# Gates, branch projections and merge with tokens on partitions; attention values placed behind fill work

## The chip, the cores and the metric

The kernel runs on one core of a Trainium2 chip. The metric is the device time of one execution in microseconds (us), as the median of three runs. A core has TensorE (PE; its weight loads are PEld), VectorE (DVE), ScalarE (ACT), GpSimd (POOL) and SyncE (SP), which run their own instruction streams and wait for one another by semaphores.

## What is computed

One layer of a diffusion backbone: 256 latent tokens and 256 context tokens, width 2048, all fp32. The part that the change touches, cut from the reference:

```python
proj = h @ w_in[l]          # columns: q 512 | kv 256 + rotary 64 | u 1024 | v 1024 | gates 4096
...
g = sigmoid(gate_in)
merged = g[..., :D_MODEL] * (attn_o @ w_br_attn) + g[..., D_MODEL:] * (sgu_o @ w_br_sgu)
x = x + g1 * (merged @ w_out)
```

`attn_o` (256 x 1024) is the output of 8 heads that attend to 512 keys; `sgu_o` (256 x 1024) is the output of the spatial gating unit. Ahead of it stand RMSNorm and a modulation by shift and scale from `silu(c) @ w_mod`; behind it a second norm, modulated by the second half of the same map (here "modulation 2": shift, gate, scale and gate of 2048 each), and a SwiGLU of width 5632.

## The kernel before

Every product of activations and weights is made of two-part numbers: a value is split into `hi` (fp32r) and `lo` (the rest, fp32r), and a product is three matmuls, hi·hi, hi·lo and lo·hi (`mm3`, all matmuls at L255). Class `W` loads weights in pieces of 512 KB (`raw`, ten buffers, on SP's queue, L234); each 512 columns of a piece become a `whi` by a copy on ACT (L241) and a `wlo` by a subtraction on DVE (L242), eight buffers of each. Four such parts, 1 MB, are one `W`. 

A product can stand in PE two ways. In the F form a 128x128 weight tile is the stationary operand and the 256 tokens move, so the result has features on its partitions: 256 columns for each matmul (`mm3`), or, in `mm_wides`, hi and lo of the tokens side by side as 512 columns for the weight's hi and 256 for its lo, which leaves two sums in one PSUM bank that the eviction adds (L641 copies on ACT, L642 adds on DVE). In the T form 128 tokens of activations are stationary and 512 columns of weights move; the result has tokens on its partitions.

The stages in the profile: input projection with modulation 1 (0 to 222 us; `in_chunk`, T items for q and v, F tiles for u and the first 4 of 32 gate tiles), the spatial gating unit and the up-projections UQ, UK, UV (222 to 346), attention (346 to 496), SGU branch projection (496 to 543), attention branch projection with the merge (543 to 591), `wout` (592 to 681), norm, SwiGLU in (692 to 1180) and out (to the end). The 28 remaining gate tiles are *fill work*: `fill_items` yields 28 half items of one `W` each, which `fill` interleaves with the stages from SGU to attention (2 in each of the 8 attention steps), then the 8 SGU branch items, whose product is multiplied into `gate_b` (L654). Attention runs 8 steps, each 4 head pairs x 2 halves of the queries: `softmax` (scores, maximum with the key row on DVE L827, exponential on ACT L833, reciprocal and scaling L834 and L835), `weighted` of the step before (four 128x128 transposes on PE L844 for each of two heads, their copy to SBUF on ACT L846, and, every second step, the products with the values and their split L290/L291), then the fill work.

Modulation 2 is *background* work: a row of 1024 columns is accumulated on DVE, 16 pieces of 512 KB each (L425, L427), at a rate per fill item. Where a row is done, four matmuls sum it over partitions, ACT copies the sums into a slot `e` (L447), POOL sends them in four DMAs to DRAM (L450) and by DMA back in the wanted layout, and `MOD2_DUE` pieces later the bias is added. The slots (`slot()`) are a pool of 60 buffers of 128x512: a new owner of a buffer waits for the last use of the old one, DMAs among them.

The order of each engine's instructions is fixed when the kernel is built, by a scheduler that goes by the order of the code, its dependences and its pools; the waits are put in then. PSUM is 4 banks "mm" and 4 banks "aux".

Of the kernel before, what the change touches and what calls it, by code (L numbers as in the profile page):

```python
# [13 lines left out]
P = 128  # L14
# [32 lines left out]
MOD2_DUE = 7  # L47
# [21 lines left out]
NB_Q, NB_V = 1, 2  # L69
NB_T = NB_Q + NB_V  # L70
NT_U, NT_G = 8, 32
KV_COLS = KV_LORA + ROPE

NT_GE = 4
NT_F = NT_U + NT_GE

# [46 lines left out]
def block_kernel(  # L123
# [277 lines left out]
    def mod2_items():  # L401


        due = []
# [209 lines left out]
    acc_v = acc_t[NB_Q:]  # L614
# [3 lines left out]
    gate_a, gate_b = acc[NT_U // 2:], []  # L618
    sgo = []
    raw_gates = list(gate_a)  # L620
# [217 lines left out]
    def weighted(p, qt):  # L838
# [22 lines left out]
    for i, (p, qt) in enumerate(steps):  # L861
# [5 lines left out]
        fill(ATT_GATES[i], ATT_RATE)  # L867
# [320 lines left out]
```

## Time and profile before

| | us |
|---|---|
| three runs | 1429.76, 1432.1, 1434.71 |
| median | 1432.1 |
| profiled execution | 1430.99 |
| span of the profiled execution | 1429.2 |
| PE busy in it | 1402.0 (98%) |
| DVE busy | 1009.3 (71%) |
| ACT busy | 766.6 (54%) |

The profiled execution lies 1.1 us under the median and 1.8 us over its own span. Busy PE is not PE at its peak: consecutive matmuls overlap, so that the cost of a matmul is read from start to start, not from its own duration.

### The profile page before, as it was taken

Reading aid. Unit: us, or ns where it says so; the run is one execution under the profiler, and the core shown is the slowest. Engines: PE = TensorE matmul, PEld = TensorE weight load, DVE = VectorE, ACT = ScalarE, POOL = GpSimd, SP = SyncE. Lnnn points to the kernel's source line nnn. Section 1 sums busy time; section 2 is a strip of 40 time slices with the busy share of each in tenths; the row PEclk is TensorE's granted clock in tenths of the full one; section 3 lists DMA queues with packets and bytes.
Section 4 is the critical chain, followed back from the end, with each engine's and each line's share of the span. In section 5 each row is a group of like instructions: output and inputs, shape, how many; then the busy total and the mean of one; then the engine's idle time right before and its main releaser. Section 6 shows DMA issues by size and latency. Waiting matters only on the chain.

```text
span 1429.2 us, 23093 instructions
## 1 busy us (share of the span) xinstructions
PE 1402.0 (98%) x8390; PEld 1189.0 (83%) x8390; DVE 1009.3 (71%) x1748; ACT 766.6 (54%) x1438; POOL 21.9 (2%) x44
## 2 busy tenths in 40 slices
PE   6999999999999999999999999999999999999998
PEld 3887899995867899888888888888888888888886
DVE  2677687984898779997766666666666667786553
ACT  4655466564645745554665555555555554444442
POOL 0000000001100000000000000000000000000000
PEclk9999999999999999999999999999999999999999
DMA  9987877674797798897444555555555568898560
GB/s 369 362 315 294 344 275 238 245 271 146 241 364 278 271 348 331 299 396 270 148 162 163 190 186 185 192 192 190 187 184 192 192 217 305 303 373 303 191 207 31
DMA packets 104019, 355.50 MB, mean 249 GB/s; under 512 B 12504, under 2 KB 14936, under 8 KB 103904
## 3 DMA queue, kind: packets, MB, share of 16 engines
q1 hardware_dynamic: 101952, 350.30, 67.5%
q0 software_dynamic: 1952, 3.72, 0.9%
q8 instruction: 66, 1.08, 0.3%
q14 instruction: 49, 0.40, 0.1%
HBM read 351.83 MB, written 2.13 MB: 248 GB/s over the span
## 4 chain that ended last, share of the span: by engine, by line
PE 91%; DMA 4%; DVE 3%; ACT 1%; issue 1%; SPq 0%; POOL 0%; DVEq 0%; ACTq 0%
PE mm L255 86%; PE ax L255 5%; DMA raw<-in_wmod_dram 2%; DVE acc L427 1%; DMA raw<-in_win_dram 1%; DVE wlo L242 1%; DMA m_d<-g 0%; ACT whi L241 0%; DMA g<-in_xT_dram 0%; ACT g L386 0%; DMA raw<-in_wbrs_dram 0%; DMA raw<-in_wkv_dram 0%; PE ax L844 0%; PE ax L359 0%; DVE g L827 0%
## 5 line engine op out<-in xcount | busy, mean ns | idle before, releaser
L241 ACT ACTIVATE whi<-raw 128x512 fp32r<-128x512 f32 (+1 forms) x900 | 556.4, 628 | 490.1 <-PE mm L255 363.4
L242 DVE TENSOR_TENSOR wlo<-raw,whi 128x512 fp32r<-128x512 f32 (+1 forms) x900 | 605.5, 687 | 271.2 <-ACT whi L241 261.7
L255 PE MATMUL mm<-g,whi 128*128 128x512 f32 (+1 forms) x2880 | 767.7, 358 | 0.0
L255 PE MATMUL mm<-g,wlo 128*128 128x256 f32 x2368 | 504.8, 281 | 0.6 <-DVE wlo L242 0.6
L255 PEld LDWEIGHTS mm<-g,wlo 128*128 128x128 f32 x2368 | 438.8, 189 | 79.4 <-issue 1.3
L255 PEld LDWEIGHTS mm<-g,whi 128*128 128x128 f32 x2880 | 447.9, 190 | 9.9 <-issue 3.3
L255 PE MATMUL mm<-whi,g 128*128 128x512 f32 (+1 forms) x1312 | 400.9, 385 | 1.9 <-ACT whi L241 1.1
L255 PEld LDWEIGHTS mm<-whi,g 128*128 128x128 f32 x1312 | 244.2, 188 | 53.6 <-issue 3.7
L255 PE MATMUL mm<-wlo,g 128*128 128x512 f32 (+1 forms) x656 | 251.0, 383 | 0.5 <-DVE wlo L242 0.5
L427 DVE SCALAR_TENSOR_TENSOR acc<-raw,silw,acc 128x1024 f32<-128x1024 f32 x120 | 153.8, 1282 | 19.3 <-DMA raw<-in_wmod_dram 18.6
L255 PEld LDWEIGHTS mm<-wlo,g 128*128 128x128 f32 x656 | 123.5, 188 | 24.9 <-DVE wlo L242 2.1
L561 DVE TENSOR_TENSOR g<-mm,g 128x512 f32<-128x512 f32 (+1 forms) x72 | 46.4, 655 | 23.4 <-PE mm L255 22.9
L255 PE MATMUL ax<-g,g 128*128 128x128 f32 (+2 forms) x224 | 45.8, 384 | 3.8 <-ACT g L846 3.4
L290 ACT ACTIVATE g<-g 128x256 fp32r<-128x256 f32 x100 | 39.0, 411 | 13.9 <-DVE g L1024 8.2
L1021 ACT ACTIVATE g<-mm 128x256 f32<-128x256 f32 x88 | 29.0, 382 | 30.9 <-PE mm L255 30.9
L1022 DVE TENSOR_TENSOR g<-mm,g 128x256 f32<-128x256 f32 x88 | 33.2, 419 | 17.3 <-ACT g L1021 17.2
L291 DVE TENSOR_TENSOR g<-g,g 128x256 fp32r<-128x256 f32 x100 | 40.2, 420 | 7.2 <-ACT g L290 7.0
L255 PEld LDWEIGHTS ax<-g,g 128*128 128x128 f32 (+1 forms) x224 | 28.4, 195 | 17.1 <-issue 9.3
L255 PE MATMUL ax<-raw,silw 128*32 128x256 f32 (+1 forms) x576 | 31.8, 358 | 4.1 <-DMA raw<-in_wmod_dram 4.0
L255 PEld LDWEIGHTS ax<-raw,silw 128*32 128x32 f32 x576 | 16.9, 109 | 17.0 <-DMA raw<-in_wmod_dram 6.6
L386 ACT ACTIVATE g<-g,m 128x256 f32<-128x256 f32 x32 | 17.6, 593 | 9.7 <-DVE m L375 5.3
L1024 DVE TENSOR_TENSOR g<-g 128x256 f32<-128x256 f32 x44 | 18.4, 419 | 1.0 <-ACT g L1023 1.0
(146 smaller groups left out, 446.2 us busy)
## 6 DMA issues: line engine op xcount, KB each, us to landing
raw<-in_wmod_dram SPq DMA_DIRECT2D x192, 512.0 KB, 6.2
raw<-in_wffi_dram SPq DMA_DIRECT2D x176, 512.0 KB, 3.2
raw<-in_wffo_dram SPq DMA_DIRECT2D x88, 512.0 KB, 4.6
raw<-in_wgate_dram SPq DMA_DIRECT2D x56, 512.0 KB, 4.9
raw<-in_win_dram SPq DMA_DIRECT2D x48, 512.0 KB, 7.1
raw<-in_wout_dram SPq DMA_DIRECT2D x32, 512.0 KB, 5.9
raw<-in_wbrs_dram SPq DMA_DIRECT2D x16, 512.0 KB, 6.3
raw<-in_wbra_dram SPq DMA_DIRECT2D x16, 512.0 KB, 7.0
```

The lines of the kernel that those rows point to most:

```text
L241: S.activation(hi[:, :e], raw[:, q:q + e], AF.Copy)
L242: V.tensor_tensor(out=lo[:, :e], in0=raw[:, q:q + e], in1=hi[:, :e].bitcast(F32), op=ALU.subtract)
L255: nc.tensor.matmul(out, lhsT, rhs, start=start, stop=stop)
L290: S.activation(dst_hi, src, AF.Copy)
L291: V.tensor_tensor(out=dst_lo, in0=src, in1=dst_hi.bitcast(F32), op=ALU.subtract)
L386: S.activation(v, v, AF.Identity, bias=m[:, 2 * jj + s:2 * jj + s + 1], scale=m[:, 2 * n + 2 * jj + s:2 * n + 1 + 2 * jj + s])
L427: V.scalar_tensor_tensor(out=acc, in0=w.raw[0], scalar=sil[:, k, 0:1], in1=acc, op0=ALU.mult, op1=ALU.add)
L561: V.tensor_tensor(out=d, in0=ps, in1=d, op=ALU.add)
L1021: S.activation(d, ps[:, 256:512], AF.Copy)
L1022: V.tensor_tensor(out=d, in0=ps[:, 0:256], in1=d, op=ALU.add)
L1024: V.tensor_tensor(out=v[:, 0:256], in0=v[:, 256:512], in1=v[:, 0:256], op=ALU.mult)
```

## The change

The gates, the two branch projections and the merge go from the F form to the T form. The first gate block (512 columns) is a T item of the input projection in place of 4 F tiles. The other 7 blocks are fill items of four `quarter`s each: 24 matmuls of 512 columns, into two banks, one for each 128 tokens; a block is evicted by two copies on ACT. The branch projections are 4 blocks of two quarters each. `merged` turns a merged block (gate-weighted sum of both branches, tokens on partitions) by 8 transposes of 128x128 on PE into the layout that `wout` wants, and splits it from PSUM; block i-1 is turned behind the matmuls of block i, the last one in `project` before its third chunk. In attention the products with the values come out of `weighted` into `values`, which stands behind the fill work of the next step (behind its 48 matmuls), and behind everything for the last head pair. The shift sums of modulation 2 are picked up at the twelfth piece of the row behind both, the other sums at the twelfth piece instead of the eighth of the next row. Bytes, number of loads and number of background pieces stay.

```diff
-MOD2_DUE = 7
+MOD2_DUE = 11
...
-NT_GE = 4
-NT_F = NT_U + NT_GE
+NB_GE = 1
+NB_T = NB_Q + NB_V + NB_GE
+NT_F = NT_U
...
-                        for f in due:
+                        for f in due + (due_far if (s, b) == (0, 1) else []):
                             f()
...
-                    due.append(lambda b=b: shift(b))
+                    due_far.append(lambda b=b: shift(b))
...
+    def quarter(ps, src, w_d, i, c, nk):
+
+        w = W(flat(w_d, i * P * WCOLS, WCOLS), WCOLS)
+        for j in range(4):
+            k = 4 * c + j
+            for tt in range(2):
+                mm3(ps[tt], rows_of(src, k, tt), w.cols(j * 512, 512), k == 0, k == nk - 1)
+
     def fill_items():
-        for i in range((NT_G - NT_GE) // 2):
-            d = slot()
-            pair = [mmbank(), mmbank()]
+        for i in range(NB_G - NB_GE):
+            ps = [mmbank(), mmbank()]
+            for c in range(KT // 4):
+                quarter(ps, hs, wgate, i * (KT // 4) + c, c, KT)
+                if c < KT // 4 - 1:
+                    yield
+            d = [slot(), slot()]
+            for tt in range(2):
+                S.activation(d[tt], ps[tt], AF.Copy)
...
-                    mm_wides(pair, [w.cols((2 * kk + h) * P) for h in range(2)], hs[k], k == 0, k == KT - 1)
...
-                V.tensor_tensor(out=v, in0=ps[:, 0:256], in1=v, op=ALU.add)
...
+                quarter(ps, sgo, wbrs, 2 * i + c, c, 8)
                 if c == 0:
                     yield
...
+            for tt in range(2):
+                V.tensor_tensor(out=gate_b[i][tt], in0=ps[tt], in1=gate_b[i][tt], op=ALU.mult)
             yield
...
-        for h in (2 * p, 2 * p + 1) if qt == 1 else ():
+
+    def values(p):
+        for h in (2 * p, 2 * p + 1):
...
         fill(ATT_GATES[i], ATT_RATE)
+        if i > 0 and qt == 0:
+            values(p - 1)
     weighted(*steps[-1])
+    values(steps[-1][0])
...
+    def merged(i):
+
+        for j in range(0, 4, 2):
+            tp = auxbank()
+            for jj in range(2):
+                for tt in range(2):
+                    nc.tensor.transpose(tp[:, jj * 256 + tt * P:jj * 256 + (tt + 1) * P],
+                                        gate_a[i][tt][:, (j + jj) * P:(j + jj + 1) * P], ident)
+            for jj in range(2):
+                t = slot(F32R)
+                split_to(t[:, 0:256], t[:, 256:512], tp[:, jj * 256:(jj + 1) * 256])
+                mg.append(t)
+
+    for i in range(4):
+        ps = [mmbank(), mmbank()]
+        for c in range(2):
+            quarter(ps, ao, wbra, 2 * i + c, c, 8)
+            background(MOD_RATE)
+        for tt in range(2):
+            g = gate_a[i][tt]
+            V.tensor_tensor(out=g, in0=ps[tt], in1=g, op=ALU.mult)
+            V.tensor_tensor(out=g, in0=g, in1=gate_b[i][tt], op=ALU.add)
+
+        if i > 0:
+            merged(i - 1)
+
...
+            if c == 2:
+                ahead()
...
+                     (lambda: merged(3)) if cb == 0 else lambda: None)
```

The scheduler's order around the change is shown at three places; names end in a running number, and the names of the two kernels don't correspond. The first is ACT in the middle of attention, where the second shift row of modulation 2 is summed: L447 is the copy of the sums, L241 the weight copies, L833 (L837 in the changed kernel) the exponential, L846 (L850) the copy of transposed weights, `DMASW` the DMAs that POOL issued. Before:

```order
L447 ACTIVATE g_4882<-ax_4877 128x256 [waits DVE_49,PE_49]
L241 ACTIVATE whi_5124<-raw_5122 128x512 [waits DMAHW5_49,DVE_49,PE_49]
L833 ACTIVATE g_4898,sm_4903<-g_4898,nb_4901,rq 128x512 [waits DVE_49]
L846 ACTIVATE g_4921<-ax_4916 128x512 [waits DMASW3_49,DMASW2_49,DMASW4_49,DMASW1_49,Activation_49]
L241 ACTIVATE whi_5128<-raw_5122 128x512 [waits PE_49]
L833 ACTIVATE g_4907,sm_4912<-g_4907,nb_4910,rq 128x512 [waits DVE_49]
L846 ACTIVATE g_4928<-ax_4923 128x512 [waits PE_49,Activation_49]
```

Changed:

```order
L447 ACTIVATE g_4585<-ax_4580 128x256 [waits DVE_49,PE_49]
L241 ACTIVATE whi_4803<-raw_4801 128x512 [waits DMAHW5_49,DVE_49,PE_49]
L837 ACTIVATE g_4601,sm_4606<-g_4601,nb_4604,rq 128x512 [waits DVE_49]
L241 ACTIVATE whi_4807<-raw_4801 128x512 [waits PE_49,Activation_49]
L241 ACTIVATE whi_4813<-raw_4811 128x512 [waits DMAHW6_49,PE_49,Activation_49]
L241 ACTIVATE whi_4817<-raw_4811 128x512 [waits PE_49,Activation_49]
L837 ACTIVATE g_4610,sm_4615<-g_4610,nb_4613,rq 128x512 [waits DMASW2_49,DMASW3_49,DMASW1_49,DMASW4_49,DVE_49,Activation_49]
L241 ACTIVATE whi_4856<-raw_4854 128x512 [waits DMAHW2_49,PE_49]
L241 ACTIVATE whi_4860<-raw_4854 128x512 [waits PE_49]
L241 ACTIVATE whi_4866<-raw_4864 128x512 [waits DMAHW3_49,PE_49]
L241 ACTIVATE whi_4870<-raw_4864 128x512 [waits PE_49]
L850 ACTIVATE g_4624<-ax_4619 128x512 [waits PE_49]
```

The wait for POOL's DMAs moved from the first copy of transposed weights to the second exponential, and ten instructions stand between the copy of the sums and that of the transposed weights where two stood.

The second place is DVE at the entry of the SGU branch projection, where background pieces (L427) and weight parts (L242) share the engine. Before:

```order
L242 TENSOR_TENSOR wlo_5697<-raw_5694,whi_5696 128x512 [waits DMAHW3_49,PE_49]
L242 TENSOR_TENSOR wlo_5701<-raw_5694,whi_5700 128x512 [waits PE_49]
L427 SCALAR_TENSOR_TENSOR acc_5453<-raw_5764,silw,acc_5453 128x1024 [waits DMAHW5_49,DVE_49]
L427 SCALAR_TENSOR_TENSOR acc_5453<-raw_5843,silw,acc_5453 128x1024 [waits DMAHW0_49,DVE_49]
L427 SCALAR_TENSOR_TENSOR acc_5453<-raw_5916,silw,acc_5453 128x1024 [waits DMAHW3_49,DVE_49]
L642 TENSOR_TENSOR g_5495<-mm_5496,g_5495 128x256 [waits Activation_49]
L642 TENSOR_TENSOR g_5495<-mm_5497,g_5495 128x256 [waits Activation_49]
L427 SCALAR_TENSOR_TENSOR acc_5453<-raw_5919,silw,acc_5453 128x1024 [waits DMAHW4_49,DVE_49]
L291 TENSOR_TENSOR g_5647<-ax_5638,g_5647 128x256 [waits Activation_49]
L427 SCALAR_TENSOR_TENSOR acc_5453<-raw_5992,silw,acc_5453 128x1024 [waits DMAHW7_49,DVE_49]
```

Changed:

```order
L242 TENSOR_TENSOR wlo_5321<-raw_5318,whi_5320 128x512 [waits DMAHW3_49,PE_49]
L839 TENSOR_SCALAR g_5113<-g_5113,sm_5118 128x512 [waits DVE_49]
L427 SCALAR_TENSOR_TENSOR acc_5070<-raw_5362,silw,acc_5070 128x1024 [waits DMAHW5_49]
L427 SCALAR_TENSOR_TENSOR acc_5070<-raw_5411,silw,acc_5070 128x1024 [waits DMAHW0_49,DVE_49]
L427 SCALAR_TENSOR_TENSOR acc_5070<-raw_5460,silw,acc_5070 128x1024 [waits DMAHW3_49,DVE_49]
L427 SCALAR_TENSOR_TENSOR acc_5070<-raw_5463,silw,acc_5070 128x1024 [waits DMAHW4_49,DVE_49]
L427 SCALAR_TENSOR_TENSOR acc_5070<-raw_5512,silw,acc_5070 128x1024 [waits DMAHW7_49,DVE_49]
L291 TENSOR_TENSOR g_5269<-ax_5260,g_5269 128x256 [waits Activation_49]
L242 TENSOR_TENSOR wlo_5325<-raw_5318,whi_5324 128x512 [waits Activation_49]
L242 TENSOR_TENSOR wlo_5331<-raw_5328,whi_5330 128x512 [waits Activation_49]
```

One weight part instead of two stands ahead of five background pieces, and they are in one row, with the next weight part behind the last of them and a split (L291).

The third is DVE at the first step of attention, where L827 (L831) takes the maximum, L831 (L835) makes the bias of the exponential, and the `wlo` are parts of the fill item's weights. Before:

```order
L827 ISA mx_4196 128x1
L831 TENSOR_TENSOR nb_4189<-mx_4187,nrq 128x1 [waits DVE_49]
L242 TENSOR_TENSOR wlo_4281<-raw_4278,whi_4280 128x512 [waits DMAHW2_49,Activation_49]
L831 TENSOR_TENSOR nb_4198<-mx_4196,nrq 128x1 [waits DVE_49]
L242 TENSOR_TENSOR wlo_4285<-raw_4278,whi_4284 128x512 [waits PE_49,Activation_49]
L242 TENSOR_TENSOR wlo_4377<-raw_4374,whi_4376 128x512 [waits DMAHW6_49,PE_49,Activation_49]
L834 RECIPROCAL sm_4191<-sm_4191 128x1 [waits Activation_49]
L835 TENSOR_SCALAR g_4186<-g_4186,sm_4191 128x512 [waits DVE_49]
L834 RECIPROCAL sm_4200<-sm_4200 128x1 [waits Activation_49]
L835 TENSOR_SCALAR g_4195<-g_4195,sm_4200 128x512 [waits DVE_49]
```

Changed:

```order
L242 TENSOR_TENSOR wlo_4056<-raw_4053,whi_4055 128x512 [waits DMAHW2_49,Activation_49]
L835 TENSOR_TENSOR nb_3982<-mx_3980,nrq 128x1 [waits DVE_49]
L242 TENSOR_TENSOR wlo_4060<-raw_4053,whi_4059 128x512 [waits PE_49,Activation_49]
L831 ISA g_4102,mx_4103<-ax_4096,g_3866 128x512
L831 ISA mx_4103 128x1
L831 ISA g_4111,mx_4112<-ax_4097,g_3868 128x512
L831 ISA mx_4112 128x1
L838 RECIPROCAL sm_3975<-sm_3975 128x1 [waits Activation_49]
L835 TENSOR_TENSOR nb_4105<-mx_4103,nrq 128x1 [waits DVE_49]
L835 TENSOR_TENSOR nb_4114<-mx_4112,nrq 128x1 [waits DVE_49]
L839 TENSOR_SCALAR g_3970<-g_3970,sm_3975 128x512 [waits DVE_49]
L242 TENSOR_TENSOR wlo_4137<-raw_4134,whi_4136 128x512 [waits DMAHW6_49,PE_49]
```

Behind the second `wlo` the next weight part followed at once; now the maxima and biases for the second half of the queries, and a reciprocal and a scaling, stand ahead of it.

## Rows read from the trace of the kernel before

**Rows 1.** The page: busy time and share of each engine.
```profile
PE 1402.0 (98%) x8390; PEld 1189.0 (83%) x8390; DVE 1009.3 (71%) x1748; ACT 766.6 (54%) x1438; POOL 21.9 (2%) x44
```
**Rows 2.** Chain that ended last: shares by engine; last link (start, us, engine, line).
```profile
PE 91%; DMA 4%; DVE 3%; ACT 1%; issue 1%; SPq 0%; POOL 0%; DVEq 0%; ACTq 0%
...
1304.16 119.74 PE mm L255 x528
```
**Rows 3.** PE's waits in the whole span: waited for, us in total, times, longest.
```profile
PE ax L255 <- ACT g L326: 4.9, 2, 4.7
...
PE ax L255 <- ACT g L846: 3.4, 2, 3.0
```
**Rows 4.** Timeline, PE, input projection: start, us, engine, line, operation [idle <-releaser].
```profile
63.02 0.40 PE L255 MATMUL mm<-g,whi 128*128 128x256 f32 x2
...
71.65 0.40 PE L255 MATMUL mm<-whi,g 128*128 128x512 f32 x1
```
**Rows 5.** Timeline, PE, wide fill items in attention.
```profile
405.86 0.62 PE L255 MATMUL mm<-g,whi 128*128 128x512 f32 x2
...
414.91 0.63 PE L255 MATMUL mm<-g,whi 128*128 128x512 f32 x2
```
**Rows 6.** Timeline, PE, the transposes of one attention step between fill matmuls.
```profile
368.06 0.62 PE L255 MATMUL mm<-g,whi 128*128 128x512 f32 x2
...
369.46 1.03 PE L844 MATMUL ax<-cst,g 128*128 128x128 f32 x8
...
371.03 0.63 PE L255 MATMUL mm<-g,whi 128*128 128x512 f32 x2
```
**Rows 7.** Windows: from:to, us, busy of PE, PEld, DVE, ACT, POOL, PEclk, DMA, GB/s.
```profile
368.00:372.00 4.00, 4.00 (x28) 3.56 (x28) 3.31 (x12) 3.21 (x8) 0.00 (x0) 1.00 0.66 213
...
426.10:429.10 3.00, 0.01 (x1) 0.01 (x1) 1.34 (x2) 0.66 (x2) 0.10 (x1) 1.00 0.91 280
...
430.00:434.00 4.00, 4.00 (x21) 3.76 (x20) 2.68 (x5) 1.52 (x6) 0.00 (x0) 0.57 0.55 164
```
**Rows 8.** Timeline, all engines, around PE's longest wait in attention.
```profile
420.64 0.38 ACT L447 ACTIVATE g<-ax 128x256 f32<-128x256 f32 x1 [3.18 <-PE ax L844]
...
421.31 1.96 POOL L450 DMA_DIRECT2D m_d<-g  x4 [14.84 <-ACT g L447]
...
428.44 0.60 ACT L846 ACTIVATE g<-ax 128x512 f32<-128x512 f32 x1 [3.07 <-DMA m_d<-g]
...
429.09 1.58 PE L255 MATMUL ax<-g,g 128*128 128x128 f32 x10 [2.99 <-ACT g L846]
```
**Rows 9.** Timeline, DVE at the first softmax of attention.
```profile
358.91 0.68 DVE L827 CUSTOM_DVE_ANT_0 g<-ax,g 128x512 f32<-128x512 f32 x1
...
360.88 1.29 DVE L242 TENSOR_TENSOR wlo<-raw,whi 128x512 fp32r<-128x512 f32 x2
```
**Rows 10.** Timeline, SP's queue, DVE and PE at the entry of the SGU branch.
```profile
491.06 0.33 SPq L234 DMA_DIRECT2D raw<-in_wmod_dram  x1
...
491.96 1.28 DVE L427 SCALAR_TENSOR_TENSOR acc<-raw,silw,acc 128x1024 f32<-128x1024 f32 x1 [0.92 <-DMA raw<-in_wmod_dram]
...
497.08 1.28 DVE L427 SCALAR_TENSOR_TENSOR acc<-raw,silw,acc 128x1024 f32<-128x1024 f32 x1 [1.64 <-DMA raw<-in_wmod_dram]
...
498.61 4.29 DVE L242 TENSOR_TENSOR wlo<-raw,whi 128x512 fp32r<-128x512 f32 x7
...
499.35 0.39 PE L255 MATMUL mm<-g,wlo 128*128 128x256 f32 x1 [0.59 <-DVE wlo L242]
```
**Rows 11.** Groups by form, DVE, 500 to 690 us: count, busy, mean ns, idle before.
```profile
L242 DVE TENSOR_TENSOR wlo<-raw,whi 128x512 fp32r<-128x512 f32 x133 | 88.2, 689 | 8.7 <-ACT whi L241 7.9 <-DMA raw<-in_wmod_dram 0.7
L427 DVE SCALAR_TENSOR_TENSOR acc<-raw,silw,acc 128x1024 f32<-128x1024 f32 x34 | 43.6, 1282 | 0.2 <-DMA raw<-in_wmod_dram 0.2
L291 DVE TENSOR_TENSOR g<-g,g 128x256 fp32r<-128x256 f32 x16 | 6.1, 423 | 0.0
...
L888 DVE TENSOR_TENSOR g<-mm,g 128x512 f32<-128x512 f32 x8 | 5.5, 690 | 0.2 <-PE mm L255 0.2
```

More of the change, by code (lines that the diff above doesn't have):

```diff
@@ L66 @@
 HOLD_AT = 0
-NB_Q, NB_V = 1, 2
-NB_T = NB_Q + NB_V
-NT_U, NT_G = 8, 32
+NB_Q, NB_V, NB_G = 1, 2, 8
+NT_U = 8
 KV_COLS = KV_LORA + ROPE
-NT_GE = 4
-NT_F = NT_U + NT_GE
+NB_GE = 1
+NB_T = NB_Q + NB_V + NB_GE
+NT_F = NT_U
 ATT_GATES = [2, 2, 2, 2, 2, 2, 2, 2]
@@ L401, in mod2_items @@
     def mod2_items():
-        due = []
+        due, due_far = [], []
         def shift(b):
@@ L612, in block_kernel @@
         todo[o].pop(0)()
-    acc_v = acc_t[NB_Q:]
+    acc_v = acc_t[NB_Q:NB_Q + NB_V]
     acc_u = acc[0:NT_U // 2]
-    gate_a, gate_b = acc[NT_U // 2:], []
+    gate_a, gate_b = acc_t[NB_Q + NB_V:], []
     sgo = []
-    raw_gates = list(gate_a)
+    raw_gates = [t for g in gate_a for t in g]
     def sigmoids():
@@ L881, in block_kernel, with project @@
     mg = []
-    for i in range(8):
-        w = W(flat(wbra, i * P * WCOLS, WCOLS), WCOLS)
-        ps = mmbank()
-        for j in range(2):
-            for k in range(8):
-                mm3(ps[:, j * 256:(j + 1) * 256], w.cols((j * 8 + k) * P), hilo(ao[k]), k == 0, k == 7)
-        V.tensor_tensor(out=gate_a[i], in0=ps, in1=gate_a[i], op=ALU.mult)
-        V.tensor_tensor(out=gate_a[i], in0=gate_a[i], in1=gate_b[i], op=ALU.add)
-        for j in range(2):
-            t = slot(F32R)
-            split_to(t[:, 0:256], t[:, 256:512], gate_a[i][:, j * 256:(j + 1) * 256])
-            mg.append(t)
-        background(MOD_RATE)
-    def project(src, w_d, cb, nk, rate, last=1):
+    def merged(i):
[9 more added lines that the diff above has]
+                mg.append(t)
+    for i in range(4):
+        ps = [mmbank(), mmbank()]
+        for c in range(2):
[7 more added lines that the diff above has]
+            merged(i - 1)
+    def project(src, w_d, cb, nk, rate, last=1, ahead=lambda: None):
         ps = [mmbank(), mmbank()]
@@ L937, in block_kernel @@
             S.activation(warm, most[1], AF.Sqrt)
-        ps = project(mg, wout, cb, KT, MOD_RATE if cb < 3 else 0.0, 2 if cb == 3 else 1)
+        ps = project(mg, wout, cb, KT, MOD_RATE if cb < 3 else 0.0, 2 if cb == 3 else 1,
+                     (lambda: merged(3)) if cb == 0 else lambda: None)
         for tt in range(2):
@@ L1126, in _layout @@
     o["wkv"] = np.concatenate([x for ks in kv_groups() for x in _chunk(kv[ks].transpose(1, 0, 2), 3 * KV_COLS)])
-    ge = OFF_GATE + NT_GE * P
-    wg = np.concatenate([wi[:, OFF_GATE + D:], wi[:, ge:OFF_GATE + D]], axis=1)
-    wg = wg.reshape(2, KT // 2, P, (NT_G - NT_GE) // 2, 2, P)
-    o["wgate"] = np.concatenate([
-        x for i in range((NT_G - NT_GE) // 2) for c in range(2) for x in _chunk(wg[c, :, :, i].transpose(1, 0, 2, 3))])
-    blocks = np.concatenate([wi[:, :OFF_KVC], wi[:, OFF_V:OFF_GATE]], axis=1).reshape(KT, P, NB_T, 512)
-    tiles = np.concatenate([wi[:, OFF_U:OFF_V], wi[:, OFF_GATE:ge]], axis=1).reshape(KT, P, NT_F, P)
+    ge = OFF_GATE + NB_GE * 512
+    o["wgate"] = _nat(np.concatenate([wi[:, OFF_GATE + D:], wi[:, ge:OFF_GATE + D]], axis=1))
+    blocks = np.concatenate([wi[:, :OFF_KVC], wi[:, OFF_V:ge]], axis=1).reshape(KT, P, NB_T, 512)
+    tiles = wi[:, OFF_U:OFF_V].reshape(KT, P, NT_F, P)
     a = {"T": blocks, "F": tiles}
@@ L1151, in _layout @@
     o["xN"] = np.ascontiguousarray(inp["x"][0])
-    pairs = [[2 * i, 2 * i + 1] for i in range(8)]
-    o["wbrs"] = _pack(inp["w_br_sgu"][0], list(range(8)), pairs)
-    o["wbra"] = _pack(inp["w_br_attn"][0], list(range(8)), pairs)
+    o["wbrs"] = _nat(inp["w_br_sgu"][0])
+    o["wbra"] = _nat(inp["w_br_attn"][0])
     o["wout"] = _nat(inp["w_out"][0])
```

23 lines of the change are left out of this document (5 added, 18 removed).

## The prediction

> **What bounds the kernel now.** I read the page's busy times first: PE works 98% of the span, DVE 71%, ACT 54% [rows 1]. Busy time can hide waits, so the chain of work that ended last comes next: 91% of it is PE, and its last link is 119.74 us of `wffo` matmuls without a break [rows 2]. That link also gives a price: 528 T matmuls of 512 columns in 119.74 us, 0.2268 us each from start to start. In the attention and merge stages the starts of PE's instructions add up to the time that passes, except where PE waits; so in these stages a microsecond of PE work taken away is a microsecond of the kernel, as long as DVE, ACT and the loads keep up. The waits are few: 4.9 us at the start, which the change doesn't touch, and 3.4 us for a copy of transposed attention weights, 3.0 of them in one piece [rows 3]. The 40 us of start and the SwiGLU are the same in both kernels.
>
> **The matmuls.** Prices from start to start: an F matmul of 256 columns 0.120 us (72 of them between 63.02 and 71.65 [rows 4]); four of the wide form (two of 512, two of 256) 0.696 us (13 such fours between 405.86 and 414.91 [rows 5]); a T matmul of 512 columns 0.2268 us [rows 2].
> - First gate block: 192 F matmuls, 23.04 us, become 96 T, 21.77: -1.27.
> - Fill gates: 14 items x 16 fours = 224 x 0.696 = 155.9 become 7 blocks x 96 = 672 x 0.2268 = 152.4: -3.5.
> - Each branch projection: 8 x 48 = 384 F, 46.08, become 4 x 48 = 192 T, 43.55: -2.53, and -5.06 for both.
>
> Together -9.8 us. The work is the same number of columns; what goes is the part of each 256-column matmul above half of a 512-column one. None of this is behind other work, since PE is the last to finish in all four places.
>
> **The transposes.** 4 blocks x 8 = 32 transposes are new, and lie on PE's path. The 8 of an attention step stand between fill matmuls: 2.97 us pass from 368.06 to 371.03 for three fours and 8 transposes [rows 6]; less 3 x 0.696 that is 0.88, or 0.110 each. 32 x 0.110 = +3.5 us. The granted clock in that stretch was 1.00, the 2.4 GHz level [rows 7], so the price holds no loss of clock.
> The Trainium skill, page "TensorE: Matmul & The Clock Gate", section on PE-mode transpose (Part 4), speaks against this step: it gives about 275 ns for a 128x128 transpose inside one kernel, and says that the full clock doesn't engage for work of that kind. An estimate by that page would be 32 x 0.275 = 8.8 us, 5.3 more than my term. The trace disagrees for the 8 that stand among matmuls, at 0.110 us and a clock of 1.00.
>
> **Evictions.** A gate block ends in two ACT copies of 512 columns instead of ACT copies and DVE additions of 256; DVE gets lighter by 28 additions. Both engines are below PE there, so I cost this at nothing. In the up-projection of queries a gate block stays half done across a `fill`, and holds two of four "mm" banks; where its second half ends, the next query tile may have to wait for its copy on ACT, one instruction of 0.6 us less what overlaps: 0 to 0.6, I take +0.4.
>
> **The wait in attention.** The sums of the second shift row are copied into slot `e` at 420.64, POOL issues four DMAs from it at 421.31 to 423.27, and ACT's next owner of that buffer, a copy of transposed weights, starts only at 428.44, with the DMA as its releaser; PE has waited 2.99 us for it [rows 8]. PE did nothing from 426.1 to 429.1 at a clock of 1.00, and behind it, from 430 to 434, the granted clock was 0.57 in the mean, partly at the 1.2 GHz level [rows 7]: 4.0 x 0.43 = 1.7 us more. So this wait costs 4.7 us. In the changed order the buffer goes to the second exponential of the next softmax (its maximum on DVE writes it first). What waits is again behind the same landing, some 7.5 us from issue; but the products with the values now stand behind 48 fill matmuls, 48 x 0.2268 = 10.9 us, that need neither. By the order the buffer is wanted on DVE some 10 us after the sums, and the DMAs have landed by then. What is late next: behind the waiting DVE instruction stand the weight parts of the next item, with a few microseconds in hand. I take -4.7, and for the small wait for a maximum in the same stage, 0.35, another -0.3; ends: 0 (the wait only moves) and -5.
> Nothing else in the moved values costs PE time: their count stays 64. The last head pair has no fill work behind it, so its values wait for the copy of transposed weights as before: 0 to 0.6, I take +0.3.
>
> **New waits.** (a) First softmax. Behind the second weight part, DVE now takes two more maxima (0.68 each [rows 9]), two biases, a reciprocal and a scaling before the next `wlo`, about 2 us. Before, that `wlo` followed at once [rows 9], with about a microsecond in hand. Bounds 0 and 2.0, taken +0.9.
> (b) Entry of the SGU branch. Five background pieces stand in a row behind one weight part where two parts stood ahead, and the last of the pieces is loaded into a buffer that the third has to free. A piece lands 6.0 us behind its issue (491.06 to 497.08 [rows 10]). From the last softmax on, that gives on DVE: third piece landed after 7.7 us and added (1.28 [rows 10]) by 9.2, last piece landed at 15.2, added at 16.4, a split of 0.42 and the part's 0.69 [rows 11]: 17.4. PE comes there after some 16 us (48 fill matmuls 10.9, 8 transposes 0.9, 16 value products 3.9). So +1.2, in place of the 0.59 that PE waits there now [rows 10]. Bounds: 0, if the loads take 5 us, and 4.5, if each of the two takes 1.6 longer.
> (c) Merge. `wout`'s third chunk wants the last merged block. Its splits on DVE come about 16.6 us behind the block's last product, PE is there after 19.1: 2.1 us in hand. DVE has for a block and its share of background 8 x 0.61 (weight parts follow each other at 4.29/7 [rows 10]) + 4 x 0.6 + 4 x 0.34 + 3 x 1.2 = 12.3 us, and PE 48 x 0.2268 + 0.88 = 11.8. (The means of DVE's instructions are 0.69, 0.42 and 1.28 [rows 11]; they overlap by about 0.08.) It falls behind by half a microsecond in each block, 2 in all; DVE already runs up with the items today, with 0.2 us of idle time ahead of 8 merge products [rows 11]. Taken 0, bounds 0 and 2.
>
> **Other edits.** In the input projection some of the -1.27 lies where PE waits for loads anyway: +0.5 (0 to 1.3). `MOD2_DUE` and the shift sums move four small DVE additions to a later place where the DMA has landed for sure: nothing. The loads of `x` and the bias rows come up to 5 us later in SP's queue, ahead of which stand the loads that wait for buffers; their users on DVE stand behind other work: 0 to 1, taken nothing.
>
> **Sum.** -9.8 + 3.5 - 4.7 - 0.3 - 0.6 (the old wait at the SGU branch) + 0.4 + 0.3 + 0.9 + 1.2 + 0.5 = -8.6 us. The profiled execution took 1430.99, so 1422.4; the median of the runs lies 1.1 above the profiled execution: 1423.5.
>
> **Rivals.**
> - The entry of the SGU branch waits long: 4.5 in place of 1.2, and behind a wait of 3 us the clock falls as it did behind the one in attention, 1.7: 5.0 more, 1428.5. For it: the load chain is two landings deep. Against it: only if each of them is late by more than 1.6 us.
> - The change doesn't do what it says: the wait for POOL's DMAs moves from ACT to the second exponential, and from there by the weight parts behind it to PE, 4.7 back: 1428.2. For it: the buffer is still handed on at once. Against it: ten ACT instructions stand between.
> - The transposes take the clock down: they come in four groups, one for each block, and if each is followed by what [rows 7] show behind the idle stretch, 4 x 1.7 = 6.8, 1430.3. Against it: clock 1.00 at the 8 in attention. By the Trainium skill's page named above, this is what one would expect, with its own figure at 1428.8.
> - Slower: DVE falls behind in the merge, so that the splits of the last merged block come late for `wout`'s third chunk. It costs from a lag of 2.1 us on; for a time over the old one the lag must be some 14 us, that is, each DVE instruction of the four blocks would take a quarter more than its row: about 1437. For it: DVE has 12.3 us for each 11.8 of PE; splits now read PSUM. Against it: two chunks of `wout` in which DVE has time.
> - Better: the new waits don't show: 2.8 less, 1420.7.
>
> **How the numbers follow.** Forecast (1421.5 to 1426) 0.57; better 0.13; SGU entry 0.11; moved wait 0.08; transposes' clock 0.05; slower 0.04; the rest, of no one cause, 0.02. The range from 1419.5 to 1429.5 takes in the first four, and leaves out the slower case, most of the transposes' case, and the ends of the others. A measurement of this kernel tells 0.3%, 4.3 us, from no change: faster is below 1427.8, slower above 1436.4. Faster: forecast, better and a part of the two cases around 1428: 0.78. Slower: 0.05. Within: 0.17.
>
> **What would show it.** In the profile after: T matmuls in fill and branches at 0.227 from start to start; 32 transposes at 0.11 with a clock of 1.00; no wait of PE at the sums of the second shift row, and no fall of the clock behind; DVE's third background piece at the SGU entry as the releaser of a wait of about 1 us. I am wrong if PE's starts in the fill work no longer add up to the time, that is, if weight parts or loads become the last to come.

## The result, and the profile after

The changed kernel takes 1423.5 us in the median of 8 runs (1421.5 to 1426.6), the kernel before 1431.3 in 8 runs beside it (1427.8 to 1434.7). The ratio is 0.9947, with a 95% interval of 0.9935 to 0.9959: 7.6 us faster, 5.9 to 9.3. The forecast was 1423.5 us, 8.6 us less than before. A second group of runs on another occasion gave 0.9956 (0.9939 to 0.9973).

The profiled execution of the changed kernel took 1426.59 (span 1424.8), the longest of the eight. A second trace, of the run e1 below, has a span of 1421.6 (1423.38), nearer to the median; where the two differ, both are named. The page of the changed kernel, beside [rows 1], and the last link of its chain, beside [rows 2]:

```profile
PE 1395.6 (98%) x7718; PEld 1154.9 (81%) x7718; DVE 999.6 (70%) x1720; ACT 764.0 (54%) x1424; POOL 21.8 (2%) x44
```
```profile
1300.44 119.74 PE mm L255 x528
```

PE still carries the chain (91% of it, as before), and the end of the kernel is the same 119.74 us, only 3.7 us earlier in this execution. What PE waits for from 230 to 500 us (line waited for: us in total, times, longest), in this trace and in that of e1:

```profile
PE ax L255 <- DVE g L706: 3.2, 2, 2.1
PE ax L255 <- ACT g L850: 2.2, 2, 1.3
PE ax L848 <- DVE g L291: 1.5, 1, 1.5
```
```profile
PE ax L255 <- DVE g L706: 2.7, 2, 1.7
PE ax L848 <- DVE g L291: 1.5, 1, 1.5
PE ax L255 <- ACT g L850: 0.4, 1, 0.4
```

The 3.0 us for the copy of transposed weights [rows 3] is no longer one piece, and the wait at the SGU branch [rows 10] is gone. But L706, the addition of the spatial bias in the gating unit, is new here, and so is the wait for the split L291: neither stood in the prediction.

A ledger compares the start times on PE, in the trace of the kernel before and in that of e1, of places that both kernels pass. The difference in brackets is what e1 gained (-) or lost (+) since the place named before it: first product of the spatial mixing 275.38 and 273.03 (-2.35); first softmax product 346.90 and 348.61 (+4.06); last transposes of attention weights 490.92 and 486.38 (-6.25); first product of the second norm 679.01 and 672.20 (-2.27); the end of the span 1429.2 and 1421.6 (-0.8). So the gain was made in the input projection, in attention and in the merge, and half of it was lost between the spatial mixing and attention, a stretch to which the prediction gave next to nothing.

### The profile page after: what moved, and what is told of

The parts are those of the page before. It is cut to its first block, busy times and chain, and to the rows that moved or that the text cites. A ratio compares the mean times of both kernels' runs of the same rounds, so it can differ in the third digit from the quotient of the medians.

```text
span 1424.8 us, 21667 instructions
## 1 busy us (share of the span) xinstructions
PE 1395.6 (98%) x7718; PEld 1154.9 (81%) x7718; DVE 999.6 (70%) x1720; ACT 764.0 (54%) x1424; POOL 21.8 (2%) x44
## 4 chain that ended last, share of the span: by engine, by line
PE 91%; DMA 4%; DVE 2%; issue 1%; ACT 1%; SPq 0%; POOL 0%; DVEq 0%; ACTq 0%
PE mm L255 84%; PE ax L255 5%; DMA raw<-in_wmod_dram 2%; DVE wlo L242 1%; DMA raw<-in_win_dram 1%; DMA raw<-in_wgate_dram 1%; PE ax L848 0%; DMA m_d<-g 0%; DVE acc L427 0%; DMA g<-in_xT_dram 0%; PE ax L359 0%; PE ax L898 0%; ACT whi L241 0%; ACT g L386 0%; DVE g L831 0%
## 5 line engine op out<-in xcount | busy, mean ns | idle before, releaser
L241 ACT ACTIVATE whi<-raw 128x512 fp32r<-128x512 f32 (+1 forms) x900 | 554.8, 627 | 480.1 <-PE mm L255 335.8
L242 DVE TENSOR_TENSOR wlo<-raw,whi 128x512 fp32r<-128x512 f32 (+1 forms) x900 | 602.2, 685 | 270.6 <-ACT whi L241 264.5
L255 PE MATMUL mm<-whi,g 128*128 128x512 f32 (+1 forms) x2080 | 640.6, 387 | 2.3 <-ACT whi L241 1.9
L255 PE MATMUL mm<-g,whi 128*128 128x512 f32 (+1 forms) x1792 | 510.7, 374 | 0.0
L255 PEld LDWEIGHTS mm<-whi,g 128*128 128x128 f32 x2080 | 388.3, 188 | 83.5 <-issue 4.5
L255 PE MATMUL mm<-wlo,g 128*128 128x512 f32 (+1 forms) x1040 | 401.1, 386 | 0.5 <-DVE wlo L242 0.5
L255 PEld LDWEIGHTS mm<-g,wlo 128*128 128x128 f32 x1600 | 295.0, 188 | 60.1 <-issue 1.2
L255 PE MATMUL mm<-g,wlo 128*128 128x256 f32 (+1 forms) x1600 | 327.4, 281 | 0.0
L255 PEld LDWEIGHTS mm<-g,whi 128*128 128x128 f32 x1792 | 279.2, 189 | 9.1 <-issue 2.9
L255 PEld LDWEIGHTS mm<-wlo,g 128*128 128x128 f32 x1040 | 195.8, 188 | 41.3 <-DVE wlo L242 2.7
L427 DVE SCALAR_TENSOR_TENSOR acc<-raw,silw,acc 128x1024 f32<-128x1024 f32 x120 | 153.5, 1279 | 26.4 <-DMA raw<-in_wmod_dram 26.1
L291 DVE TENSOR_TENSOR g<-g,g 128x256 fp32r<-128x256 f32 x84 | 34.1, 420 | 6.1 <-ACT g L290 5.8
L837 ACT ACTIVATE g<-g,nb,rq 128x512 f32<-128x512 f32 x16 | 13.0, 811 | 15.0 <-DVE nb L835 14.9
```

The costliest lines, as they stand in the source:

```text
L241: S.activation(hi[:, :e], raw[:, q:q + e], AF.Copy)
L242: V.tensor_tensor(out=lo[:, :e], in0=raw[:, q:q + e], in1=hi[:, :e].bitcast(F32), op=ALU.subtract)
L255: nc.tensor.matmul(out, lhsT, rhs, start=start, stop=stop)
L291: V.tensor_tensor(out=dst_lo, in0=src, in1=dst_hi.bitcast(F32), op=ALU.subtract)
L427: V.scalar_tensor_tensor(out=acc, in0=w.raw[0], scalar=sil[:, k, 0:1], in1=acc, op0=ALU.mult, op1=ALU.add)
L837: exps.append(S.activation(t, t, AF.Exp, bias=nb, scale=rq[:, col:col + 1], accum_out=sm))
```

## The experiments

The ratios are to the kernel before on the same chip, with 95% intervals.

**e1, the changed kernel again.**

> The changed kernel as it is, beside the kernel before on this chip. Theory (the sum of the prediction's parts): ratio near 0.9947, and the waits that its first trace shows are there again: PE behind the spatial bias addition (L706) 3.2 us in two waits near 277 and 283 us, behind the copies of transposed weights (L850) 0.9 near 438 and for the split (L291) 1.5 near 444. Rival: these waits belong to that one execution, which took 1426.6 where the median is 1423.5; then a second trace lacks some 3 us of them.

1423.9 us, 0.9956 (0.9939 to 0.9973). The waits for L706 and L291 are there again (above); of L850 0.4 is left of 2.2. So the new waits belong to the kernel, and their sum varies by some 2 us between executions (the first trace also started its first product of the input projection about 1.2 us later). One of them has a cause of its own: of the 2.2 us for L850 in the first trace 1.3 stand near 402 us, behind weight copies for which ACT had waited 4.9 us until a load of gate weights landed. In e1 ACT waited 2.9 us there and PE not at all.

**e2, the products with the values back ahead of the fill work.**

```diff
-    def values(p):
-        for h in (2 * p, 2 * p + 1):
+        for h in (2 * p, 2 * p + 1) if qt == 1 else ():
...
-        if i > 0 and qt == 0:
-            values(p - 1)
     weighted(*steps[-1])
-    values(steps[-1][0])
```

> The changed kernel with the products with the values back in weighted(), ahead of the fill work, as before; all else as changed. Theory of the prediction: the wait of 3.0 us and the fall of the clock (1.7) behind the second shift row's sums return, so 4.7 us slower than the changed kernel: ratio 0.998 to before. Rival A (what the trace of the changed kernel suggests): of the 4.7 us 2.4 were only moved to later waits of PE, so that putting the values back costs 2.3 us: ratio 0.9963. Rival B: with the blocks of 48 matmuls in one bank pair the wait does not come back at all: 0.9947.

1429.0 us, 0.9988 (0.9974 to 1.0002): 5.1 slower than e1, the size that the prediction gave. The longest of PE's waits from 230 to 510 us, and a window (from:to, us, busy of PE, PEld, DVE, ACT, POOL, PEclk, DMA, GB/s) around and behind the last of them, which ended at 496.9:

```profile
PE ax L255 <- DVE g L706: 2.8, 2, 1.7
PE ax L255 <- ACT g L850: 1.6, 2, 1.2
PE mm L255 <- DVE wlo L242: 1.2, 1, 1.2
PE mm L255 <- ACT whi L241: 0.8, 1, 0.8
```
```profile
496.00:500.00 4.00, 3.11 (x7) 2.48 (x8) 4.00 (x8) 3.19 (x6) 0.00 (x0) 0.60 1.00 363
```

The size came, the place did not. The wait for the sums' DMAs is 1.2 us here, not 3.0, and the clock doesn't fall behind it. The other part stands at the entry of the SGU branch: 2.0 us of waits for the first weight parts, and then 4 us at a mean clock of 0.60, 4.0 x 0.40 = 1.6 more. That is the mechanism of the prediction's first rival, in a kernel in which it had not been looked for. Against the kernel before, e2 is the change without the move: 1.1 us faster, with an interval that takes in no difference at all.

**e3, the kernel before with the values moved and nothing else.**

```diff
-        for h in (2 * p, 2 * p + 1) if qt == 1 else ():
+    def values(p):
+        for h in (2 * p, 2 * p + 1):
...
         fill(ATT_GATES[i], ATT_RATE)
+        if i > 0 and qt == 0:
+            values(p - 1)
     weighted(*steps[-1])
+    values(steps[-1][0])
```

> The kernel before with only the move of the products with the values behind the next step's fill work. Theory of the prediction: -4.7 us, ratio 0.9967, and no wait of PE near 429 us. Rival A: -2.3 us, ratio 0.9984, with PE waits of some 2.4 us further back. Rival B: no gain, 1.000: the wait for POOL's DMAs stays on ACT's copy and PE meets it behind the fill work.

1425.7 us against 1430.1, 0.9965 (0.9954 to 0.9977): -4.4 us against -4.7 expected; rivals A (0.9984) and B lie outside. PE's waits from 230 to 500 us:

```profile
PE ax L844 <- DVE g L291: 1.5, 1, 1.5
PE ax L255 <- ACT g L846: 0.6, 2, 0.4
PE ax L255 <- DVE g L702: 0.2, 1, 0.2
```

Before, the waits in this stretch and the loss of clock were 3.4 + 0.6 + 0.3 + 1.7 = 6.0; here 2.3 are left, at a clock of 1.00 from 400 to 500 us. That is 3.7 us less by the trace. So more than half of the whole gain is this one move, and it needs no other layout.

**e4, each group of four transposes done twice.**

```diff
-            for jj in range(2):
-                for tt in range(2):
+            for jj, tt in [(jj, tt) for _ in range(2) for jj in range(2) for tt in range(2)]:
```

> The changed kernel with each group of four transposes of a merged block done twice into the same bank (64 in place of 32). Theory of the prediction: 32 x 0.110 = 3.5 us more than the changed kernel, clock at 1.00 around them: ratio 0.9972. Rival: by the Trainium skill, page TensorE: Matmul & The Clock Gate, section Part 4, transposes take about 0.275 us and the full clock does not engage: 8.8 us or more, ratio 1.0009 or higher.

1427.3 us, 0.9983 (0.9974 to 0.9993): 3.4 more than e1 for 32 transposes, 0.106 each. Window around the first doubled group, same columns:

```profile
556.00:562.00 6.00, 6.00 (x36) 5.18 (x35) 5.70 (x13) 3.29 (x8) 0.00 (x0) 1.00 0.90 357
```

The clock stayed at 1.00, its 2.4 GHz level. A cost of 0.275 us for each transpose, by which the expectation reckons its rival (ratio 1.0009 or higher), lies outside the interval. What that figure is in this kernel is said in the part on the prediction.

**e5, no background pieces in the query up-projection.**

```diff
-GATE_RATE = 2.2
+GATE_RATE = 0.0
```

> The changed kernel with no background pieces of modulation 2 in the query up-projection's fill (GATE_RATE 0; the same pieces come later). Theory: PE's two waits of 2.7 us in all for the spatial bias addition (L706) come from pieces (L427) that stand ahead of it on DVE and wait for their loads; with none there, both go, 2.7 us faster than the changed kernel, ratio 0.9937, unless the pieces cost as much where they go. Rival: L706 is late for DVE's weight parts, which stay; then the waits stay and the ratio is 0.9956.

1433.2 us, 1.0015 (1.0006 to 1.0024): 9 us slower than the changed kernel, and yet the cause was the right one. PE's waits from 230 to 680 us, and the first stretch of `wout`'s last block:

```profile
PE ax L255 <- DVE acc L427: 10.7, 1, 10.7
PE mm L255 <- DVE wlo L242: 0.9, 1, 0.9
PE ax L255 <- ACT g L850: 0.3, 1, 0.3
```
```profile
642.00:653.00 11.00, 0.27 (x2) 0.03 (x1) 11.00 (x14) 2.44 (x6) 0.00 (x0) 0.63 1.03 372
```

L706 is gone from the list, so without the pieces ahead of it on DVE PE doesn't wait for it; of the waits in attention 0.3 us is left. But the 9 pieces that were put off came due together in `wout`: DVE is busy for all of 11 us, PE stands still for 10.7, and the granted clock falls.

A run with the edits of e5, e6 and e7 at once, e8, was to gain 7.5 us on the changed kernel (ratio 0.990). It took 1432.9 us, 1.0015 (1.0006 to 1.0023), as e5 alone: PE meets the same wait of 10.7 us in `wout`, so that nothing of what the other two edits gave ahead of it was left.

**e6, a buffer of their own for the sums; e12, its control.** There was no room for the buffer, so a slot was given up.

```diff
-    gp = ctx.enter_context(tc.tile_pool(name="gp", bufs=60))
+    gp = ctx.enter_context(tc.tile_pool(name="gp", bufs=59))
...
-                e = slot()
+                e = wp.tile([P, 256], F32, tag="esum", name=f"esum{uid()}", bufs=1)
```

> The changed kernel with the sums of modulation 2 in a buffer of their own in place of a slot (and 59 slots in place of 60, for room). Theory: the waits that are left in attention behind the second shift row's sums (0.4 us for L850 and 1.5 for L291 in the traces of the changed kernel) are the old wait of 3 us in its new place, since the second maximum (L831) still waits for POOL's DMAs; without that, they go: 1.9 us faster, ratio 0.9943. Rival: the split L291 is late for the background pieces ahead of it on DVE; then the 1.5 us stay.

> The changed kernel with 59 slots in place of 60 and nothing else. Theory: the 5.6 us that PE lost near 406 us in the run with a buffer of its own for the sums came from the slot that was given up, which moved the first shift addition (L408) on DVE 37 instructions ahead of where it was; here it stands there too, so PE waits near 406 again and the ratio is near 0.998. Rival: it came from the buffer of its own; then no such wait and 0.9956.

e6: 1429.9 us, 0.9983 (0.9973 to 0.9994). e12, with 59 slots alone: 1431.2 us, 0.9999 (0.9984 to 1.0014). Waits of PE from 230 to 510 us in e6, then in e12, each with the DVE rows (idle before, and its releaser) that stand ahead of its waits (for L706, 2.4 and 2.8 us, as in the changed kernel):

```profile
PE ax L255 <- DVE mx L831: 5.9, 2, 5.6
...
```
```profile
393.49 0.17 DVE L408 TENSOR_TENSOR sh<-sh,prm 128x8 f32<-128x8 f32 x1 [5.25 <-DMA sh<-m_d]
```
```profile
PE ax L255 <- DVE mx L831: 4.6, 3, 3.7
...
PE ax L848 <- DVE g L291: 1.5, 1, 1.5
```
```profile
393.40 0.17 DVE L408 TENSOR_TENSOR sh<-sh,prm 128x8 f32<-128x8 f32 x1 [3.32 <-DMA sh<-m_d]
...
464.58 0.17 DVE L408 TENSOR_TENSOR sh<-sh,prm 128x8 f32<-128x8 f32 x1 [5.06 <-DMA sh<-m_d]
```

In both, one slot less moved the addition of the first shift row (L408) ahead on DVE, to where its DMA has not landed. DVE then works without a gap to the maximum (405.5 and 405.4) for which PE waits, and in this order that maximum stands 10.7 us of DVE's work behind the other one of its step, where in e1 it follows at once. So DVE's idle time reaches PE almost whole: 3.3 us become a wait of 3.7, 5.25 one of 5.6.

e6 also lacks the waits for L291 and L850, as the theory says, and no instruction of DVE or ACT waits for the sums' DMAs there. e12 is no control for that: its second shift row is summed some 28 us later than in e6 (POOL's issue at 453.6 and at 425.9), and its wait for L291 stands behind the second addition L408, which waits 5.1 us for the DMA that brings the sums back. So the slot as the cause of the 1.5 us rests on the order of DVE in the changed kernel's own trace, shown further down, and on e6, whose order differs in other places too. What the buffer is worth without the lost slot wasn't tried.

**e7, the key norm's sums in fewer groups.** Eight matmuls, each with a result on 32 partitions, sum the squares of the keys' heads.

```diff
-        if h % 4 == 3:
+        if h in (5, 7):
+            g = h // 7
             for q in range(4):
-                mm(kss[32 * q:32 * q + 32, :], unit[:, 32 - h // 4:64 - h // 4], ksq[h - 3 + q], False, h >= 4)
+                mm(kss[32 * q:32 * q + 32, :], unit[:, 32 - g:64 - g], ksq[4 * g + q], False, g == 1)
```

> The changed kernel with the first group of the key norm's four 32-row sums written two heads later, so that PE has fewer of them alone. Theory: in the trace of the changed kernel the eight stand in seven groups, each of about 0.98 us whether it holds one or three, where the kernel before had five; in four groups 2.9 us go: ratio 0.9936. Rival: the single ones are covered by the matmuls around them; then the ratio stays at 0.9956.

1420.4 us, 0.9925 (0.9912 to 0.9939), 3.5 under e1 (4.4 by the two ratios). The timeline's rows of these matmuls (each stands as two records) in the kernel before, in the changed kernel and in e7:

```profile
330.51 1.05 PE L255 MATMUL ax<-g,unit 128*32 128x512 f32 x4
332.85 1.05 PE L255 MATMUL ax<-g,unit 128*32 128x512 f32 x2
334.95 1.05 PE L255 MATMUL ax<-g,unit 128*32 128x512 f32 x2
339.55 1.85 PE L255 MATMUL ax<-g,unit 128*32 128x512 f32 x8
```
```profile
331.97 1.04 PE L255 MATMUL ax<-g,unit 128*32 128x512 f32 x2
333.37 1.04 PE L255 MATMUL ax<-g,unit 128*32 128x512 f32 x2
335.48 1.04 PE L255 MATMUL ax<-g,unit 128*32 128x512 f32 x2
337.83 1.04 PE L255 MATMUL ax<-g,unit 128*32 128x512 f32 x2
342.19 1.06 PE L255 MATMUL ax<-g,unit 128*32 128x512 f32 x6
343.60 1.04 PE L255 MATMUL ax<-g,unit 128*32 128x512 f32 x2
```
```profile
330.45 1.04 PE L255 MATMUL ax<-g,unit 128*32 128x512 f32 x2
334.38 1.06 PE L255 MATMUL ax<-g,unit 128*32 128x512 f32 x6
338.31 1.06 PE L255 MATMUL ax<-g,unit 128*32 128x512 f32 x6
339.73 1.05 PE L255 MATMUL ax<-g,unit 128*32 128x512 f32 x2
```

One alone takes the 1.04 us that three together take, about 0.98 from start to start. The changed kernel has six groups (not seven, as the expectation says), five of them of one; the kernel before took 4.7 us for all, the changed one 5.9. So the change lost 1.2 us here, through the order of PE alone, and e7 takes off two groups, 2.0 us by these rows; the measured difference holds that within its interval, and what more there may be is not explained.

**e9, the sums of modulation 2 picked up as before.**

```diff
-MOD2_DUE = 11
+MOD2_DUE = 7
...
-                    due_far.append(lambda b=b: shift(b))
+                    due.append(lambda b=b: shift(b))
```

> The changed kernel with the sums of modulation 2 picked up as before (eighth piece, the shift rows' too). Theory of the prediction: the later place of these additions is worth nothing, so ratio 0.9956 as the changed kernel. Rival, from the run with a buffer of its own for the sums, where the addition of the shift (L408) came some 37 instructions earlier on DVE and held DVE for 5.3 us, PE for 5.6: picked up early, the first shift row's addition waits for its DMA ahead of a maximum of the softmax; PE loses some 5 us near 400 us, ratio 0.9991.

1422.9 us, 0.9946 (0.9927 to 0.9965): as the changed kernel. The later pick-up is worth nothing that can be measured, as forecast.

**e10 and e11, towards a better kernel**, both with e7's groups.

```diff
-GATE_RATE = 2.2
+GATE_RATE = 0.0
...
-SGU_RATE = 0.0
+SGU_RATE = 1.1
```

> The changed kernel with the key norm's sums in fewer groups and the 8.8 background pieces of the query up-projection put ahead into the gating unit's fill (SGU_RATE 1.1, GATE_RATE 0), so that none stands at the spatial bias additions and none is put off. Theory: the 2.7 us of waits for L706 go on top of the gain of the groups, about 1417.7, ratio 0.9905. Rival: the pieces wait for their loads in their new place and take gate weights with them; then no better than 1420.4, ratio 0.9925.

```diff
-GATE_RATE = 2.2
-ATT_RATE = 2.9
+GATE_RATE = 0.0
+ATT_RATE = 3.1
...
-MOD_RATE = 1.4
+MOD_RATE = 1.6
```

> As the run beside it, but the pieces are put off and spread (ATT_RATE 3.1, MOD_RATE 1.6), so that the last row is due in wout when it was. Theory: the waits for L706 go, and the 10.7 us for the last rows in wout, which the run with GATE_RATE 0 had, do not come: about 1417.7, ratio 0.9905. Rival: DVE, already 37 of 40 us busy from 380 to 420 us, falls behind in attention, and the gain is lost.

e10: 1417.1 us against 1430.5, 0.9903 (0.9885 to 0.9920), faster than both kernels, and about 3 us under e7. e11: 1431.4, 1.0009 (0.9998 to 1.0021): the waits for L706 are gone there too, but waits in attention and 6.8 us in `wout` take their place. PE's waits in e10 from 230 to 510 us:

```profile
PE ax L848 <- DVE g L291: 1.5, 1, 1.5
PE ax L255 <- ACT g L850: 0.7, 1, 0.7
```

The pieces stand ahead of the spatial bias now, none is put off, and what is left is the moved wait for POOL's DMAs. Not all of the 3 us need be the waits for L706: the key norm's sums stand in three groups here, one fewer than in e7.

## Why the prediction was right, and where only its sum was

**The matmuls: right.** To the first mixing product, with the same start of PE's work, the terms give -1.27 and, for two gate blocks, -1.0; -2.35 was measured. From the last attention transposes to the second norm they give -5.06 + 3.5 - 0.6 = -2.2; -2.27 was measured. The term did not come everywhere: the gate block between the mixing and the first softmax, worth -0.5 by the prediction, gave nothing. From start to start, without the waits, the 208 matmuls of 256 columns and 136 of 512 there took 57.8 us before, and the 144 and 168 of e1 took 57.8 as well. The price of a T matmul beside fill work is the one taken: 10.91 us for 48 in a link of the chain, 0.2273 each.

```profile
408.66 10.91 PE mm L255 x48
```

The +0.5 for the first gate block under loads didn't come.

**The transposes: right, slightly dear.** The first merged block and the matmul behind it, then all 32 transposes as a group (count, busy, mean ns of one, idle before):

```profile
560.26 1.03 PE L898 MATMUL ax<-cst,g 128*128 128x128 f32 x8
561.05 0.48 PE L255 MATMUL mm<-whi,g 128*128 128x512 f32 x1
```
```profile
L898 PE MATMUL ax<-cst,g 128*128 128x128 f32 x32 | 4.2, 274 | 0.0
```

0.79 us for 8, 0.099 each against 0.110; e4 says 0.106. The rival of the clock did not come: the clock stayed at 1.00. The Trainium skill (page "TensorE: Matmul & The Clock Gate", Part 4: PE-mode transpose) gives about 275 ns for one transpose inside a kernel. This trace agrees, with 274 ns in the mean from the start of one to its own end (an end that the profile models). The prediction's estimate of 32 x 0.275 misread that figure as a cost: the next transpose starts 0.1 us behind, while the one before still runs. The page's other statement, that the full clock doesn't engage for such work, is not tested here: at most 16 transposes stand in a row (e4), between matmuls and at a clock that was full already.

**The wait in attention: size right, its end wrong.** The prediction said that the DMAs land before the new owner of the buffer wants it, some 10 us behind the sums. They don't: DVE stands ready for it 5.4 us behind the copy of the sums (423.7 to 429.1), and the last landing comes 8.1 us behind POOL's first issue. In the changed kernel:

```profile
424.40 1.97 POOL L450 DMA_DIRECT2D m_d<-g  x4 [13.33 <-ACT g L447]
...
432.51 0.69 DVE L831 CUSTOM_DVE_ANT_0 g<-ax,g 128x512 f32<-128x512 f32 x1 [3.37 <-DMA m_d<-g]
```
```profile
437.73 4.83 PE L255 MATMUL ax<-g,g 128*128 128x128 f32 x24 [0.87 <-ACT g L850]
...
444.09 1.10 PE L848 MATMUL ax<-cst,g 128*128 128x128 f32 x8 [1.53 <-DVE g L291]
```
```profile
443.61 0.75 DVE L291 TENSOR_TENSOR g<-ax,g 128x256 fp32r<-128x256 f32 x2
```

DVE waits 3.4 us for the same landing, and has no gap from there to L291, which comes 3.4 us after ACT's copies that it needs (done at 440.2). The 48 matmuls hide that until 436.9, and PE then loses 0.9 and 1.5, without a fall of the clock. So the second rival, that the wait moves, was half true: 2.4 of 4.7 us stayed in this trace, 1.9 in e1. e3 still gives -4.4: the fall of the clock, 1.7 [rows 7], went whole, and with it the wait at the SGU branch, 0.6 [rows 10], which the prediction had as a term of its own.

**The new waits: none of the four came, and two came that weren't there.** First softmax (+0.9), SGU entry (+1.2), query banks (+0.4) and last values (+0.3): no wait of PE at any of them. At the SGU entry the mis-sized term is the load. SP's last background piece ahead of the branch, and its user on DVE:

```profile
487.98 0.33 SPq L234 DMA_DIRECT2D raw<-in_wmod_dram  x1
```
```profile
492.48 1.29 DVE L427 SCALAR_TENSOR_TENSOR acc<-raw,silw,acc 128x1024 f32<-128x1024 f32 x1 [3.20 <-DMA raw<-in_wmod_dram]
```

4.5 us from issue to use, where 6.0 was taken from one row of before. In their place stand 2.7 to 3.2 us at L706 and 1.2 us for the split groups of the key norm. The step that failed is the part on evictions: it took DVE as free in the gate blocks' stretches because it is below PE on the mean, and did not look at what DVE has ahead of the spatial bias, or at what PE has between the mixing products. PE's two waits in the changed kernel, and DVE ahead of the second:

```profile
276.87 0.71 PE L255 MATMUL ax<-g,g 128*128 128x128 f32 x4 [1.09 <-DVE g L706]
...
283.16 0.71 PE L255 MATMUL ax<-g,g 128*128 128x128 f32 x4 [2.14 <-DVE g L706]
```
```profile
281.15 1.29 DVE L427 SCALAR_TENSOR_TENSOR acc<-raw,silw,acc 128x1024 f32<-128x1024 f32 x1 [2.15 <-DMA raw<-in_wmod_dram]
...
282.68 0.42 DVE L706 TENSOR_TENSOR g<-ax,g 128x256 f32<-128x256 f32 x1
```

The second wait is that of a background piece for its load. For the first, a piece that waits for nothing stands ahead of L706 (275.20 to 276.48), as one did before (275.67); but before, PE had seven matmuls of another product between its first 16 mixing products and the next four (277.08 to 278.00), and now these follow at once. Without the pieces, in e5 and e10, both waits go.

**The sum.** Three of its figures don't follow from their own terms or rows, and none decides anything: the margin of 2.1 us in the merge is 2.5 by its two times (19.1 and 16.6), the 9.2 us for the third piece at the SGU entry is 9.0 (7.7 + 1.28), and the wait for a maximum, 0.35, is 0.29 in the trace of before. Forecast were 3.3 us of small losses (2.8 of new waits, 0.5 of the gate block); 5.8 came (2.7 at L706, 1.2 in the key norm, 1.9 of the moved wait), and none but a part of the last had been named. With what was measured the sum reads -9.8 + 3.2 (32 x 0.099) - 6.0 (waits and clock of before in this stretch, as under e3) + 5.8 = -6.8, where e1's span is 7.6 shorter; the other 0.8 is the ledger's last stretch, in which both kernels do the same. In the ledger +0.7 is left over ahead of attention and -0.7 in it; 0.5 of the first is the gate block named above, and why it gave nothing, and the rest, stays open. That the total came out at 1423.5 is therefore partly luck: the large terms held, while the small ones were wrong one by one and left the gain only 1.0 us too large. The other luck is in the base: the median of before that the forecast started from, 1432.1 of three runs, lies 0.8 above that of the eight, 1431.3.

**The slower rival** (the merge's DVE late for `wout`) didn't show: no wait of PE stands between 500 and 670 us.

## What to carry to other kernels

A wait of the bounding engine can be taken away without shortening what it waits for, by putting independent work of that engine between; look then at where the released engine next waits for the same thing, since some of it comes back there. When instructions are reordered by a scheduler, look through the whole order of each engine, also where the diff touches nothing: here 1.2 and 2.7 us were lost in stages whose own code the diff doesn't touch, and one buffer less in a pool cost about as much as the whole change gained (e12). Background work is put best where its loads are surely there and nothing short stands behind it: moved ahead it gave 3 us in this kernel (e10 against e7), put off it cost 9 (e5).

## What the runs showed of the hardware

An fp32 matmul with 32 stationary and 512 moving columns takes about 0.98 us of PE from start to start when it stands alone, and three of them that write different groups of 32 partitions take the same time together (rows under e7), as do four in the trace of e10 (331.23 to 332.23). So scattered ones cost three to four times as much here. 128x128 fp32 transposes among matmuls cost 0.10 to 0.11 us from start to start, about half of a 512-column matmul, though each lasts 0.27 us, and leave the granted clock at 1.00. The granted clock fell behind PE's wait of 3.0 us before (0.57 over 4 us [rows 7]) and behind the two waits at the SGU entry in e2 (0.60 over 4 us); behind PE's waits of 5.6 us in e6 and 3.7 in e12 it fell too (0.59 and 0.50 from 406 to 410 us). Behind the changed kernel's waits from 230 to 500 us, the longest of 2.1, it stayed at 1.00.
